# Rotation tables through one transposition in the pair of keys and values, widened by loads from DRAM, and only the rotated rows of a q result stored raw

## The chip, the cores and the metric

The kernel runs on one core of a Trainium2 chip. The metric is the device time of one execution in microseconds (us), lower is better. Before the change three executions took 894.03, 894.17 and 894.5 us; the median is 894.17.

The core has engines that run side by side, each with its own row of instructions: TensorE (PE: matrix products and transpositions), VectorE (DVE), ScalarE (ACT) and GpSimd (POOL). SyncE (SP) computes nothing here; it issues most transfers (DMAs). An engine takes its instructions strictly in order, so one that has to wait holds up all that stand behind it on the same engine.

## The reference

One block of an audio encoder over 1024 time steps and 1024 channels, all in float32. Cut to what matters:

```python
h = rmsnorm(x, norm_g[l])
proj = h @ w_in[l]                               # 1024 x 7424
q, k, v, za, u, vs, zs, gm = jnp.split(proj, IN_SPLITS, axis=-1)
q = partial_rope(q.reshape(B, S, 16, 64), pos)   # 16 heads of 64
k = partial_rope(k.reshape(B, S, 2, 64), pos)    # 2 heads
v = v.reshape(B, S, 2, 64)
a = window_sink_attention(q, k, v, att_sinks[l]) # chunks of 64, window 128
a = (a * silu(za)) @ w_att_out[l]
sgo = (chunked_spatial_gating(gelu(u), gelu(vs), ...) * silu(zs)) @ w_sg_out[l]
ga, gs = jnp.split(sigmoid(gm + b_merge[l]), 2, axis=-1)
x = rmsnorm(x + (ga * a + gs * sgo) @ w_o[l], final_g)

def partial_rope(x, pos):          # ROPE_DIM = 16: 8 angles
    ang = pos[:, None] * inv_freq[None, :]
    x1, x2, rest = x[..., :8], x[..., 8:16], x[..., 16:]
    return concatenate([x1*cos - x2*sin, x2*cos + x1*sin, rest], -1)
```

The rotation touches the first 16 of the 64 channels of a head, and uses a table of 1024 times x 8 angles of cosines and one of sines.

## The kernel before

**Pairs.** The product with `w_in` is made in pairs. A pair (`gemm_pair`) makes two blocks of 128 output channels x 1024 times with the channels on the partitions and the times along the row. It is one step of Strassen's scheme: seven products in the order b11, t1, t2, b21, t3, b22, t4, each of 12 matmuls (four slices of the sum, times three for a float32 split into a high and a low part). Keys `(n, 0..6)` name the seven weight parts of pair n. What a pair needs is made one pair ahead on the other engines: SP loads the raw weights into `wr` (`copy_to`, L212; `wr` has three buffers in rotation), DVE makes four sums of two weight blocks (tile `s`, L262 to L265: `a21+a22`, that plus `a11`, `a11+a21`, and `a12` plus the second sum), ACT rounds a part to its high half (`wh`, L176), DVE subtracts for the low half (`wl`, L177). The results of a pair are assembled from two PSUM tiles by DVE (L392, L397, L401, one for each result but the last). In the trace the product t4 writes the PSUM tile `ps_mm` that L397 has to have read.

**Stages around the change.** After the gMLP pairs comes the pair of keys and values (185.0 to 204.8 us on PE), then four pairs of q, which start on PE at 204.78 (`m=0`), 224.38 (`m=2`), 244.38 (`m=4`) and 263.42 us (`m=6`); each makes two blocks of two heads. Then come the pairs of the gate z (the first from 282.46 us), and from about 304 us the attention, step by step between the products of further pairs.

**Work beside the pairs.** `gemm_pair` calls a hook between its products. In the pair of keys and values `hook` takes steps out of the list `late`; in the q pairs `part_of_q` advances generators in `steps_of_q`: `rope_tables` in the pair `m=2`, `rotate_keys` and `rotate(0)` from `m=4`, later `first_loads` and `rotate(1)`. The order in which the instructions stand on each engine is then set by a scheduler that works on the whole program, so a changed instruction can shift others that the diff does not touch.

**The tables.** `rope_tables` loads `cos` and `sin` (times on the partitions, 16 per time step) as two DMAs into `both` (L1212), spreads the 8 angles over 8 heads by eight copies on DVE (L1218, `wide`), turns each table by four transpositions on PE (L1225, one group of four per table) and copies the PSUM tile to `tab0` and `tab1` on ACT (L1226). `tab` has 128 rows: two halves of the times, 8 heads, 8 angles.

**Results of a q pair.** `finish` stores each of the four results of a pair, 128 x 512 floats (256 KB), to `q_raw` in DRAM (`put`, L520) and the split result to `q_hl` (`split_q`, L1240 on DVE and the DMA at L1245). `rotate` later loads from `q_raw` the first 16 rows of each head (L1294), multiplies them with the tables on DVE (L1314 and after), and writes the rotated rows into `q_hl`. `rotate_keys` (L1258, L1275 to L1284) does the same for the keys out of `k_raw`, into which only the 16 rows of each of the two heads are stored (`keys_of`). The attention loads its queries from `q_hl`.

Of the kernel before, what the change touches and what calls it, by code (L numbers as in the profile page):

```python
# [24 lines left out]
F32 = mybir.dt.float32  # L25
# [5 lines left out]
P = 128  # L31
D = 1024
S = 1024
KC = D // P
HALF = 512
NT = S // P
HD = 64
# [15 lines left out]
def hybrid_tile(  # L53
# [16 lines left out]
    nc = tc.nc  # L70
# [24 lines left out]
    def xtile():  # L95
        return mtile([P, HALF], F32, "x", 5)
# [16 lines left out]
    ident = const.tile([P, P], F32, name="ident")  # L113
# [18 lines left out]
    q_raw = scratch("q_raw")  # L132
# [2 lines left out]
    k_dr = scratch("k_dr", (P, 4, S))  # L135
    v_dr = scratch("v_dr", (NT, P, 2, 3 * HD))
    s1_dr = scratch("s1_dr")
    z_dr = scratch("z_dr")
    gs_dr = scratch("gs_dr")
    ga_dr = scratch("ga_dr")  # L140
# [70 lines left out]
    def copy_to(dst, src):  # L211
        nc.sync.dma_start(dst, src)  # L212
# [11 lines left out]
    def split_next():  # L224

        if not units:
            begin_job()
        if not units:
            return
        halves, keys = units.pop(0)  # L230
        if keys[0][1] == 2:
            make_sums(term_of_x11[0] if done[0] <= 4 else None)
        hi = mtile([P, D], F32R, "wh", 3)
        lo = mtile([P, D], F32R, "wl", 3)
        if isinstance(halves, list):
            for c, half in enumerate(halves):
                split(hi[:, half_of(c)], lo[:, half_of(c)], half)
        else:
            wide = halves.shape[1]
            first = split(hi[:, 0:wide], lo[:, 0:wide], halves)  # L240
            if keys[0] == (done[0] - 1, 6) and done[0] > LAST_OF_Q + 2:
                if bounds:
                    sums_behind.append(first)
                else:
                    make_sums(first)
        of_units.append(hi_of[-1])
        for c, key in enumerate(keys):
# [106 lines left out]
    def product(acc, part, form, fresh, last=True):  # L354
        wh, wl = part
        bh, bl = form
        for k in range(4):
            ks = slice(k * P, (k + 1) * P)
            for n, (lt, rt) in enumerate(
                ((wh[:, ks], bh[:, k, :]), (wh[:, ks], bl[:, k, :]), (wl[:, ks], bh[:, k, :]))  # L360
            ):
                nc.tensor.matmul(  # L362
                    acc,
                    lt,
                    rt,
                    start=fresh and k == 0 and n == 0,
                    stop=k == 3 and n == 2,
                    skip_group_check=True,
                )

    def gemm_pair(b, finish, hook=lambda: None, second="o"):

        n = done[0]
        done[0] += 1
        acc = bank("mm")[:]
        x11, x12, x22 = xtile(), xtile(), xtile()
        product(acc, ready[n, 0], b["b11"], True)
        pace[0] = nc.scalar.copy(x11[:], acc)  # L380
        hook()
        t5 = bank("o")[:]
        product(t5, ready[n, 2], b["t1"], True)
        pace[0] = nc.scalar.mul(x22[:], t5, -1.0)
        hook()
        product(acc, ready[n, 3], b["t2"], False)
        pace[0] = nc.scalar.copy(x12[:], acc)
        split_next()
        hook()
        t2 = bank(second)[:]  # L390
        product(t2, ready[n, 1], b["b21"], True)
        term[0] = term_of_x11[0] = nc.vector.tensor_add(x11[:], x11[:], t2)  # L392
        finish(0, 0, x11, x11[:], 1.0)
        split_next()
        hook()
        product(acc, ready[n, 4], b["t3"], False)
        term[0] = nc.vector.tensor_sub(x22[:], x22[:], acc)  # L397
        finish(1, 1, x22, x22[:], 1.0)
        hook()
        product(t5, ready[n, 5], b["b22"], False)  # L400
        term[0] = nc.vector.tensor_add(x12[:], x12[:], t5)  # L401
        finish(0, 1, x12, x12[:], 1.0)
        split_next()
        hook()
        product(acc, ready[n, 6], b["t4"], False)
        finish(1, 0, xtile(), acc, -1.0)
        split_next()
        hook()
# [107 lines left out]
    def place(dst, m, half):  # L516
        return dst[m * P : (m + 1) * P, half_of(half)]

    def put(dst, m, half, src, queue=nc.sync):
        queue.dma_start(place(dst, m, half), src)  # L520
# [22 lines left out]
    pool = outer.enter_context(tc.tile_pool(name="mixing", bufs=1))  # L543
# [527 lines left out]
    late = []  # L1071
    in_twos = set()

    def hook():
        if len(late) == 1 and late[0] in in_twos:
            return
        for _ in range(2):
            if late:
                late.pop(0)()
# [57 lines left out]
    for m in range(0, KC, 2):  # L1137

        def finish(i, half, q, src, sign, m=m):
            nc.scalar.activation(q[:], src, AF.Gelu, scale=sign)  # L1140
            late.append(lambda: mix(m + i, half, q))
            in_twos.add(late[-1])
# [11 lines left out]
    pool = stage.enter_context(tc.tile_pool(name="keys", bufs=1))  # L1154
# [32 lines left out]
    def finish(i, half, q, src, sign):  # L1187
        if sign < 0:
            nc.scalar.mul(q[:], src, sign)
        (values_of if i else keys_of)(half, q)  # L1190

    gemm_pair(hb, finish, hook)
    stage.close()

# [4 lines left out]
    pool = stage.enter_context(tc.tile_pool(name="queries", bufs=1))  # L1199
    split_pool = stage.enter_context(tc.tile_pool(name="split", bufs=1))  # L1200
    SC = -(HD**-0.5)
    tables = []

    def rot_tile():
        return mtile([P, HALF], F32, "rot", 5, pool)

    both = rot_tile()[:, 0 : 2 * NT * 16].rearrange("p (f t d) -> p f t d", f=2, t=NT)

    def rope_tables():

        for f, src in enumerate((cos, sin)):
            nc.sync.dma_start(both[:, f], src)  # L1212
        yield
        for src in (both[:, 0, :, 0:8], both[:, 1, :, 8:16]):
            tab = mtile([P, HALF], F32, f"tab{len(tables)}", 1, pool)
            wide = rot_tile()
            for i in range(4):
                nc.vector.tensor_copy(  # L1218
                    wide[:, i * P : (i + 1) * P].rearrange("p (a h d) -> p a h d", a=2, h=8),
                    src[:, i : i + 5 : 4, :].unsqueeze(2).broadcast_to([P, 2, 8, 8]),  # L1220
                )
            yield
            pt = bank("tp")
            for i in range(4):
                nc.tensor.transpose(pt[:, i * P : (i + 1) * P], wide[:, i * P : (i + 1) * P], ident[:])  # L1225
            nc.scalar.copy(tab[:], pt[:])  # L1226
            tables.append(tab)
            yield

# [103 lines left out]
    for m in range(0, KC, 2):  # L1333

        def finish(i, half, q, src, sign):
            if sign < 0:
                nc.scalar.mul(q[:], src, sign)
            put(q_raw, m + i, half, q[:])
            rows = slice((m + i) * P, (m + i + 1) * P)
            split_q(q[:], [(slice(0, P), q_hl[:, rows, half_of(half)].rearrange("a p t -> p a t"))])  # L1340

        if m == 2:
            steps_of_q.append(rope_tables())
        if m == 4:
            steps_of_q.append(rotate_keys(0))
            steps_of_q.append(rotate(0, 3))
        gemm_pair(hb, finish, part_of_q)
# [62 lines left out]
    pool = stage.enter_context(tc.tile_pool(name="attention", bufs=1))  # L1410
# [234 lines left out]
    pool = stage.enter_context(tc.tile_pool(name="later", bufs=1))  # L1645
# [384 lines left out]
    for p in range(4):  # L2030
        n, t, acc, x11 = N_PAIRS + p, T_ORDER[p], accs[p], firsts[p]
# [191 lines left out]
```

## Time and profile before

The profiled execution is one execution by itself, with a time of its own.

| what | us |
|---|---|
| median of three executions | 894.17 |
| the profiled execution | 894.7 |
| its span, first to last instruction | 892.9 |
| PE busy in it | 881.7 |
| DVE busy | 684.9 |
| ACT busy | 580.1 |

The execution's time is 1.8 us longer than the span; that is what lies around the instructions. PE is busy in 99% of the span, so what other engines do appears in the time only where PE waits for it, or where PE itself has more or less to do.

A line of a timeline in the profile gives the start in us, the duration in us, engine, line of the code, operation, the tile written and the tiles read, the shapes, and a count; behind it, in brackets, the idle time of the engine ahead of it and what ended it. `DVE x L397` in a list of waits is the DVE instruction of line 397 that writes the tile `x`. SPq is SP's queue of DMA issues: its duration is that of the issue, not of the transfer.

### The profile page before, as it was taken

How to read it: one execution, taken by the hardware profiler on the slowest of the kernel's cores; microseconds unless marked ns; L12 is line 12 of the kernel's file. 1: busy time of each engine (PE TensorE's matmuls, PEld its weight loads, DVE VectorE, ACT ScalarE, POOL GpSimd, SP SyncE). 2: the span in 40 equal slices, each digit the busy share in tenths (PEclk: the TensorE clock that was granted, in tenths of full speed). 3: DMA queues.
4: the chain of work that ended last, by engine and by line, in shares of the span. 5: the costliest groups of instructions: out<-in, count | busy, mean ns of one | idle time of the engine just before them, and what ended most of it. 6: DMA issues, size and time to landing. Idle time of an engine off the chain costs nothing.

```text
span 892.9 us, 13164 instructions
## 1 busy us (share of the span) xinstructions
PE 881.7 (99%) x4117; PEld 731.4 (82%) x4117; DVE 684.9 (77%) x1362; ACT 580.1 (65%) x1189; POOL 150.9 (17%) x217
## 2 busy tenths in 40 slices
PE   8999999999999999999999999999999999999996
PEld 6888888888888888888888888888888888888885
DVE  7979966566686778888878888847796578579886
ACT  6875533334445489989989899955685385467443
POOL 3322222203030001111211011101121121110012
PEclk9999999999999999999999999999999999999999
DMA  9998888958778667888786789989899789998533
GB/s 332 211 268 222 268 206 172 176 153 265 250 252 286 214 189 189 210 185 195 179 236 210 237 225 222 250 290 383 308 289 376 276 231 258 298 307 282 179 119 118
DMA packets 131410, 212.40 MB, mean 238 GB/s; under 512 B 12778, under 2 KB 59882, under 8 KB 131340
## 3 DMA queue, kind: packets, MB, share of 16 engines
q1 hardware_dynamic: 108808, 148.62, 50.0%
q0 software_dynamic: 22384, 62.67, 31.6%
q8 instruction: 33, 0.54, 0.2%
q14 instruction: 37, 0.30, 0.1%
q10 hardware_dynamic: 148, 0.27, 0.1%
HBM read 146.37 MB, written 86.11 MB: 260 GB/s over the span
## 4 chain that ended last, share of the span: by engine, by line
PE 92%; ACT 3%; DVE 2%; issue 1%; DMA 1%; POOL 0%; SPq 0%; ACTq 0%; DVEq 0%
PE ps_mm L362 42%; PE ps_o L362 24%; PE ps_tp L362 7%; PE ps_sc L362 3%; PE ps_tp L793 2%; PE ps_o L793 2%; PE ps_mm L793 2%; PE ps_tp L1515 2%; PE ps_sc L1442 2%; PE ps_tp L1112 2%; PE ps_o L1550 1%; PE ps_sc L793 1%; ACT wh L176 1%; DVE wl L177 1%; PE ps_o L1555 1%
## 5 line engine op out<-in xcount | busy, mean ns | idle before, releaser
L176 ACT CAST wh<-s 128x1024 fp32r<-128x1024 f32 (+1 forms) x79 | 79.4, 1006 | 75.2 <-PE ps_mm L362 23.5
L177 DVE TENSOR_TENSOR wl<-wr,wh 128x512 fp32r<-128x512 f32 (+1 forms) x77 | 72.0, 937 | 58.0 <-ACT wh L176 57.9
L177 DVE TENSOR_TENSOR wl<-s,wh 128x1024 fp32r<-128x1024 f32 (+1 forms) x79 | 92.9, 1176 | 11.8 <-ACT wh L176 11.7
L176 ACT CAST wh<-wr 128x512 fp32r<-128x512 f32 (+1 forms) x77 | 63.0, 819 | 55.9 <-PE ps_mm L362 31.5
L1448 ACT COPY sl<-ps_sc 128x384 f32<-128x384 f32 (+2 forms) x128 | 51.8, 456 | 9.9 <-DVE sm L1454 9.9
L362 PE MATMUL ps_o<-T_t1h,wh 128*128 128x512 f32 x148 | 57.9, 391 | 0.0
L362 PE MATMUL ps_o<-T_t1h,wl 128*128 128x512 f32 x148 | 57.7, 390 | 0.0
L362 PE MATMUL ps_o<-T_t1l,wh 128*128 128x512 f32 x148 | 57.6, 389 | 0.0
L1470 ACT ACTIVATE pr<-pr,sm 128x192 f32<-128x192 f32 (+2 forms) x128 | 56.2, 444 | 0.1
L1454 DVE CUSTOM_DVE_ANT_0 pr<-sl,nsink_sb 128x192 f32<-128x192 f32 (+2 forms) x128 | 48.0, 399 | 9.9 <-ACT sl L1448 8.8
L362 PE MATMUL ps_mm<-T_b11h,wh 128*128 128x512 f32 x140 | 54.9, 392 | 0.0
L362 PE MATMUL ps_mm<-T_t3h,wh 128*128 128x512 f32 x140 | 54.7, 390 | 0.0
L362 PE MATMUL ps_mm<-T_b11l,wh 128*128 128x512 f32 x140 | 54.6, 390 | 0.0
L362 PE MATMUL ps_mm<-T_t2h,wh 128*128 128x512 f32 x140 | 54.6, 390 | 0.0
L362 PE MATMUL ps_mm<-T_b11h,wl 128*128 128x512 f32 x140 | 54.6, 390 | 0.0
L362 PE MATMUL ps_mm<-T_t3h,wl 128*128 128x512 f32 x140 | 54.6, 390 | 0.0
L362 PE MATMUL ps_mm<-T_t2l,wh 128*128 128x512 f32 x140 | 54.6, 390 | 0.0
L362 PE MATMUL ps_mm<-T_t3l,wh 128*128 128x512 f32 x140 | 54.5, 390 | 0.0
L362 PE MATMUL ps_mm<-T_t2h,wl 128*128 128x512 f32 x140 | 54.5, 389 | 0.0
L362 PE MATMUL ps_mm<-T_t4h,wh 128*128 128x512 f32 x136 | 53.2, 391 | 0.3 <-DVE x L397 0.3
L362 PE MATMUL ps_mm<-T_t4h,wl 128*128 128x512 f32 x136 | 53.0, 390 | 0.0
L362 PE MATMUL ps_mm<-T_t4l,wh 128*128 128x512 f32 x136 | 52.9, 389 | 0.0
(432 smaller groups left out, 2448.5 us busy)
## 6 DMA issues: line engine op xcount, KB each, us to landing
wr<-in_w_dram SPq DMA_DIRECT2D x86, 256.0 KB
sums<-in_w_dram POOLq DMA_DIRECT2D x20, 512.0 KB, 7.0
s<-sums SPq DMA_DIRECT2D x20, 512.0 KB
q_hl<-qhl SPq DMA_DIRECT2D x16, 512.0 KB
q<-q_hl SPq DMA_DIRECT2D x64, 128.0 KB
y_dr<-x POOLq DMA_DIRECT2D x28, 256.0 KB, 6.8
g<-in_w_dram POOLq DMA_DIRECT2D x12, 512.0 KB, 6.8
wr<-in_w_dram SPq DMA_DIRECT2D x11, 512.0 KB
```

The costliest lines, as they stand in the source:

```text
L176: hi_of.append(nc.scalar.copy(hi, src))
L177: lo_of.append(nc.vector.tensor_sub(lo, src, hi.bitcast(F32)))
L362: nc.tensor.matmul(acc, lt, rt, start=fresh and k == 0 and n == 0, stop=k == 3 and n == 2, skip_group_check=True,)
L793: mm = nc.tensor.matmul(acc[:], lt, rt, start=fresh and k == 0 and n == 0, stop=stops and k == 3 and n == terms[-1], skip_group_check=True,)
L1112: nc.tensor.matmul(pm[:, t * P : (t + 1) * P], xh[:, half * 4 + t, g * P : (g + 1) * P], bias[-1][1][:, g % 4, :], start=True, stop=True,)
L1442: nc.tensor.matmul(sc, q_of[:, c, i * P : (i + 1) * P], kt[:, :, lo:hi], start=True, stop=True)
L1448: copies.append(nc.scalar.copy(two, sc))
L1454: nc.vector.tensor_tensor_reduce(v, two[:, 0, :], two[:, 1, :], 1.0, nsk[:, i : i + 1], op0=ALU.add, op1=ALU.min, accum_out=nmax[:, c, i : ...
L1470: e = nc.scalar.activation(v, v, AF.Exp, bias=nmax[:, c, i : i + 1], scale=-1.0, accum_out=sums[:, c, i : i + 1])
L1515: nc.tensor.transpose(dst, pr[:, i, block * P : block * P + width], ident[:])
L1550: nc.tensor.matmul(po[:, first], va[1][:, vs], a[:, n, first], start=n == 0, stop=n == 1, skip_group_check=True)
L1555: nc.tensor.matmul(po[:, cs], vb[c][:, vs], b[c][:], start=t == 0, stop=True, skip_group_check=True)
```

## The change

Three things change.

1. The tables are turned once, in narrow form. In the pair of keys and values two DMAs load `cos` and `sin` into `both` (`load_tables`), two copies on DVE pack the 8 cosines and 8 sines of the eight time blocks into one 128 x 128 tile (`pack_tables`), one transposition on PE turns it, ACT copies the result to `turned`, and two DMAs issued by ACT write it to DRAM as `rope_dr` (2 x 8 x 1024) (`turn_tables`). These steps stand in `late`.
2. The spreading over 8 heads is done by four loads in the pair `m=2` that read the 8 rows of a half eight times (64 rows x 512 each, straight into `tab0` and `tab1`). The eight copies, the eight transpositions and the two ACT copies there are gone.
3. Of each q result only the first 16 rows of either head are stored to `q_raw`: two DMAs of 16 x 512 (32 KB) in place of one of 128 x 512.

```diff
+    rope_dr = scratch("rope_dr", (2, 8, S))
...
+    both = mtile([P, 2, NT, 16], F32, "both", 1, pool)
+    narrow, turned = (mtile([P, P], F32, tag, 1, pool) for tag in ("narrow", "turned"))
+
+    def load_tables():
+        for f, src in enumerate((cos, sin)):
+            nc.sync.dma_start(both[:, f], src)
+
+    def pack_tables():
+        for f in range(2):
+            nc.vector.tensor_copy(
+                narrow[:, 64 * f : 64 * f + 64].rearrange("p (n d) -> p n d", n=NT),
+                both[:, f, :, 8 * f : 8 * f + 8],
+            )
+
+    def turn_tables():
+        pt = bank("tp")
+        nc.tensor.transpose(pt[:, 0:P], narrow[:], ident[:])
+        nc.scalar.copy(turned[:], pt[:, 0:P])
+        for f in range(2):
+            nc.scalar.dma_start(rope_dr[f].rearrange("d (n p) -> n d p", n=NT), turned[64 * f : 64 * f + 64])
...
+    late += [load_tables, pause, pause, pause, pack_tables, pause, pause, turn_tables]
     gemm_pair(hb, finish, hook)
...
     def rope_tables():
-        for f, src in enumerate((cos, sin)):
-            nc.sync.dma_start(both[:, f], src)
-        yield
-        for src in (both[:, 0, :, 0:8], both[:, 1, :, 8:16]):
-            tab = mtile([P, HALF], F32, f"tab{len(tables)}", 1, pool)
-            wide = rot_tile()
-            for i in range(4):
-                nc.vector.tensor_copy(
-                    wide[:, i * P : (i + 1) * P].rearrange("p (a h d) -> p a h d", a=2, h=8),
-                    src[:, i : i + 5 : 4, :].unsqueeze(2).broadcast_to([P, 2, 8, 8]),
+        for f in range(2):
+            tab = mtile([P, HALF], F32, f"tab{f}", 1, pool)
+            for half in range(2):
+                nc.sync.dma_start(
+                    tab[64 * half : 64 * half + 64],
+                    rope_dr[f][:, half_of(half)].unsqueeze(0).broadcast_to([8, 8, HALF]),
                 )
-            yield
-            pt = bank("tp")
-            for i in range(4):
-                nc.tensor.transpose(pt[:, i * P : (i + 1) * P], wide[:, i * P : (i + 1) * P], ident[:])
-            nc.scalar.copy(tab[:], pt[:])
             tables.append(tab)
             yield
...
-            put(q_raw, m + i, half, q[:])
+            for g in range(2):
+                at = slice(g * HD, g * HD + 16)
+                copy_to(q_raw[(m + i) * P + g * HD : (m + i) * P + g * HD + 16, half_of(half)], q[at])
```

The scheduler's order changes with it. Line numbers after the change are higher by 1 up to the pair of keys and values and by 15 in the code of the q pairs (L262 becomes L263, L397 becomes L398, L1245 becomes L1260). Buffer numbers differ between the two orders.

The first place is PE. Before, a group of four transpositions stands between the products t2 and b21 of the pair `m=2`, and a second one between t3 and b22 (`T_t2h`, `T_b21h` and so on are the high and low parts of the activations):

```order
755 L362 MATMUL ps_mm_314_2059<-T_t2h_132_693,wh_304_2019 128x512
756 L362 MATMUL ps_mm_314_2059<-T_t2l_133_694,wh_304_2019 128x512
757 L362 MATMUL ps_mm_314_2059<-T_t2h_132_693,wl_305_2020 128x512
758 L1225 MATMUL ps_tp_323_2115<-ident_71,rot_320_2093 128x128 x4
759 L362 MATMUL ps_o_324_2121<-T_b21h_13_142,wh_300_1973 128x512
760 L362 MATMUL ps_o_324_2121<-T_b21l_14_143,wh_300_1973 128x512
```

After it, one transposition stands between b21 and t3 of the pair of keys and values, and none in the q pairs:

```order
597 L363 MATMUL ps_o_275_1782<-T_b21h_13_143,wh_250_1615 128x512
598 L363 MATMUL ps_o_275_1782<-T_b21l_14_144,wh_250_1615 128x512
599 L363 MATMUL ps_o_275_1782<-T_b21h_13_143,wl_251_1616 128x512
600 L1209 MATMUL ps_tp_279_1809<-ident_71,narrow_266_1728 128x128
601 L363 MATMUL ps_mm_268_1730<-T_t3h_139_755,wh_257_1688 128x512
602 L363 MATMUL ps_mm_268_1730<-T_t3l_140_756,wh_257_1688 128x512
```

Eight transpositions in two groups became a single one, some 150 rows earlier.

The second place is SP, from the middle of the pair `m=2` into `m=4`. Before, the raw weights of one later pair (`wr_339` and `wr_340`, four loads each) are spread between the stores of the results:

```order
75 L212 DMA wr_339_2227<-in_w_dram 128x2x128 x4
76 L1258 DMA rot_348_2257<-k_raw_90 16x1x512
77 L520 DMA q_raw_88<-x_315_2060 128x512
78 L212 DMA wr_340_2228<-in_w_dram 128x2x128 x2
79 L1245 DMA q_hl_89<-qhl_325_2136 128x2x512
80 L520 DMA q_raw_88<-x_317_2062 128x512
81 L1245 DMA q_hl_89<-qhl_330_2165 128x2x512
82 L520 DMA q_raw_88<-x_316_2061 128x512
83 L212 DMA wr_340_2228<-in_w_dram 128x2x128 x2
84 L1258 DMA rot_348_2257<-k_raw_90 16x1x512
85 L1245 DMA q_hl_89<-qhl_332_2190 128x2x512
86 L520 DMA q_raw_88<-x_335_2215 128x512
```

After it, the second raw tile (now `wr_339`) follows all stores of the pair `m=2`, the one of `qhl_335` included:

```order
72 L213 DMA wr_338_2227<-in_w_dram 128x2x128 x3
73 L213 DMA q_raw_88<-x_318_2076 16x512 x2
74 L213 DMA wr_338_2227<-in_w_dram 128x2x128
75 L1260 DMA q_hl_89<-qhl_327_2145 128x2x512
76 L213 DMA q_raw_88<-x_320_2078 16x512 x2
77 L1260 DMA q_hl_89<-qhl_330_2169 128x2x512
78 L213 DMA q_raw_88<-x_319_2077 16x512 x2
79 L1260 DMA q_hl_89<-qhl_331_2189 128x2x512
80 L213 DMA q_raw_88<-x_334_2214 16x512 x2
81 L1260 DMA q_hl_89<-qhl_335_2218 128x2x512
82 L213 DMA wr_339_2228<-in_w_dram 128x2x128 x4
```

The loads of the second tile moved from two places between the stores to one place behind them.

The third place is DVE in the pair `m=4`, which reads that tile. Before, the four sums stand ahead of the low part of `wr_311` and of the result x (L392):

```order
268 L1240 SCALAR_TENSOR_TENSOR qhl_336_2218<-x_335_2215,qhl_336_2218 128x256 x2
269 L262 TENSOR_TENSOR s_341_2237<-wr_340_2228 128x512
270 L1276 TENSOR_TENSOR rot_350_2259<-rot_348_2257,tab1_328_2145 128x512
271 L263 TENSOR_TENSOR s_341_2237<-s_341_2237,wr_339_2227 128x512
272 L1278 TENSOR_TENSOR rot_349_2258<-rot_349_2258,rot_350_2259 128x512
273 L264 TENSOR_TENSOR s_342_2238<-wr_339_2227,wr_340_2228 128x512
274 L265 TENSOR_TENSOR s_342_2238<-wr_339_2227,s_341_2237 128x512
275 L177 TENSOR_TENSOR qhl_354_2300<-rot_349_2258,qhl_354_2300 128x512
276 L177 TENSOR_TENSOR wl_353_2296<-wr_311_2048,wh_352_2295 128x512
277 L392 TENSOR_TENSOR x_344_2240<-x_344_2240,ps_o_355_2311 128x512
```

After it, two of the sums (now L263 and L265) follow that low part, and L398 (L397 before) stands eight rows behind them:

```order
267 L178 TENSOR_TENSOR wl_352_2296<-wr_314_2064,wh_351_2295 128x512
268 L263 TENSOR_TENSOR s_340_2237<-wr_339_2228 128x512
269 L265 TENSOR_TENSOR s_341_2238<-wr_338_2227,wr_339_2228 128x512
270 L393 TENSOR_TENSOR x_343_2240<-x_343_2240,ps_o_354_2311 128x512
271 L1290 TENSOR_TENSOR rot_348_2258<-rot_346_2256,tab0_321_2092 128x512
272 L178 TENSOR_TENSOR wl_357_2333<-wr_338_2227,wh_356_2332 128x1024
273 L1291 TENSOR_TENSOR rot_349_2259<-rot_347_2257,tab1_323_2109 128x512
274 L1297 TENSOR_TENSOR rot_346_2256<-rot_346_2256,tab1_323_2109 128x512
275 L1293 TENSOR_TENSOR rot_348_2258<-rot_348_2258,rot_349_2259 128x512
276 L1296 TENSOR_TENSOR rot_347_2257<-rot_347_2257,tab0_321_2092 128x512
277 L398 TENSOR_TENSOR x_345_2242<-x_345_2242,ps_mm_342_2239 128x512
```

The sums moved behind, and the other two (L264 and L266 now) come six and eight rows after the last row shown. On PE, three matmuls of the next pair's b11 also stand ahead of this pair's t4 now.

More of the change, by code (lines that the diff above doesn't have):

```diff
@@ L1190, in finish, with pause @@
         (values_of if i else keys_of)(half, q)
+    both = mtile([P, 2, NT, 16], F32, "both", 1, pool)
[15 more added lines that the diff above has]
+            nc.scalar.dma_start(rope_dr[f].rearrange("d (n p) -> n d p", n=NT), turned[64 * f : 64 * f + 64])
+    def pause():
+        pass
+    late += [load_tables, pause, pause, pause, pack_tables, pause, pause, turn_tables]
     gemm_pair(hb, finish, hook)
@@ L1205, in rot_tile @@
         return mtile([P, HALF], F32, "rot", 5, pool)
-    both = rot_tile()[:, 0 : 2 * NT * 16].rearrange("p (f t d) -> p f t d", f=2, t=NT)
     def rope_tables():
-        for f, src in enumerate((cos, sin)):
-            nc.sync.dma_start(both[:, f], src)
-        yield
-        for src in (both[:, 0, :, 0:8], both[:, 1, :, 8:16]):
-            tab = mtile([P, HALF], F32, f"tab{len(tables)}", 1, pool)
-            wide = rot_tile()
-            for i in range(4):
-                nc.vector.tensor_copy(
-                    wide[:, i * P : (i + 1) * P].rearrange("p (a h d) -> p a h d", a=2, h=8),
-                    src[:, i : i + 5 : 4, :].unsqueeze(2).broadcast_to([P, 2, 8, 8]),
-                )
-            yield
-            pt = bank("tp")
-            for i in range(4):
-                nc.tensor.transpose(pt[:, i * P : (i + 1) * P], wide[:, i * P : (i + 1) * P], ident[:])
-            nc.scalar.copy(tab[:], pt[:])
+        for f in range(2):
[4 more added lines that the diff above has]
+                    rope_dr[f][:, half_of(half)].unsqueeze(0).broadcast_to([8, 8, HALF]),
+                )
             tables.append(tab)
```

## The prediction

> **What bounds the kernel.** I read the head of the page first, then the chain that ended last, PE's list of waits, and the busy time in the pair `m=4`, 243.9 to 263.1 us (columns: PE, PEld, DVE, ACT, POOL, clock, DMA share, GB/s).
>
> ```profile
> span 892.9 us, 13164 instructions
> PE 881.7 (99%) x4117; PEld 731.4 (82%) x4117; DVE 684.9 (77%) x1362; ACT 580.1 (65%) x1189; POOL 150.9 (17%) x217
> PE 92%; ACT 3%; DVE 2%; issue 1%; DMA 1%; POOL 0%; SPq 0%; ACTq 0%; DVEq 0%
> PE ps_tp L1515 <- DVE pr L1493: 1.7, 6, 0.3
> PE ps_mm L362 <- DVE x L397: 0.3, 1, 0.3
> 243.90:263.10 19.20, 19.20 (x86) 15.90 (x85) 15.32 (x26) 8.66 (x13) 4.49 (x8) 1.00 0.77 252
> ```
>
> PE is busy 881.7 of 892.9 us and carries 92% of the chain. Its longest wait in sum outside the start is 1.7 us, far behind the stages changed here; in the pair `m=4` it is busy for all 19.20 us at full clock. So work taken off DVE, ACT or the DMA engines gives nothing here. PE work taken away counts whole, and each new wait of PE counts whole. PE's 11.2 us of idle time bound what a lighter load elsewhere could still give.
>
> **The change part by part.**
>
> *Transpositions.* I take their price from the distance of the starts of the pairs, not from their durations, because matmuls overlap. The starts, and PE around the first group:
>
> ```profile
> 224.38 0.39 PE L362 MATMUL ps_mm<-T_b11h,wh 128*128 128x512 f32 x1
> 244.38 0.39 PE L362 MATMUL ps_mm<-T_b11h,wh 128*128 128x512 f32 x1
> 263.42 0.39 PE L362 MATMUL ps_mm<-T_b11h,wh 128*128 128x512 f32 x1
> 282.46 0.39 PE L362 MATMUL ps_mm<-T_b11h,wh 128*128 128x512 f32 x1
> ...
> L1225 PE MATMUL ps_tp<-ident,rot 128*128 128x128 f32 x8 | 1.2, 272 | 0.0
> ...
> 232.54 0.60 PE L1225 MATMUL ps_tp<-ident,rot 128*128 128x128 f32 x4
> 232.90 0.48 PE L362 MATMUL ps_o<-T_b21h,wh 128*128 128x512 f32 x1
> 233.21 0.40 PE L362 MATMUL ps_o<-T_b21l,wh 128*128 128x512 f32 x1
> ...
> 332.55 0.82 PE L1515 MATMUL ps_tp<-ident,pr 128*128 128x128 f32 x6
> 333.12 0.43 PE L1442 MATMUL ps_sc<-k,q 128*128 128x384 f32 x1
> ```
>
> The pairs `m=4` and `m=6` take 263.42 - 244.38 = 19.04 and 282.46 - 263.42 = 19.04 us, which is 84 matmuls at 0.227. The pair `m=2` takes 244.38 - 224.38 = 20.00. It has the two groups and nothing else more on PE, so a group costs 0.96 / 2 = 0.48 us. The rows agree: four transpositions take 232.90 - 232.54 = 0.36, and the matmul behind them lasts 233.21 - 232.90 = 0.31 in place of 0.227, together 0.44. In the attention a group of six takes 333.12 - 332.55 = 0.57, so one more transposition costs about 0.10 us, and a single one 0.48 - 3 x 0.10 = 0.18. In all 0.18 - 0.96 = **-0.78 us**. The bounds: 7 x 0.10 = -0.7 if the start of a group cost nothing, and 7 x 0.272 = -1.90 if each gave back its own duration. I take -0.78, because it comes from starts of pairs, which are what moves the end.
>
> *Copies on DVE and ACT.* Eight copies of 1.17 us in all and two ACT copies go, two copies and one ACT copy come in the pair before. They cost and give nothing: PE waited for neither. In the pair of keys and values the transposition stands behind b21, past the middle of 19.8 us; the loads of `cos` and `sin` are issued at its start and have several us.
>
> *The tables by DRAM.* Two stores of 32 KB issued by ACT, and four loads of 128 KB by SP early in the pair `m=2`. Their user is the first product with a table on DVE, which stood at 242.46 us and now stands around 255. The lead is some 20 us, so nothing; if the path took longer than that, DVE would wait and PE behind it.
>
> *Stores to `q_raw`.* 3 MB less is written. PE does not wait for these bytes. On SP's queue 16 issues become 32 small ones:
>
> ```profile
> L520 SPq DMA_DIRECT2D q_raw<-x x16: 320/338/740, 217.5 to 285.6; - x16
> L1294 SPq DMA_DIRECT2D rot<-q_raw x8: 567/586/749, 248.0 to 295.0; - x8
> L212 SPq DMA_DIRECT2D k_raw<-x x4: 308/478/1906, 197.3 to 203.3; - x4
> SPq L212 <- DVE wl L177: 14.4, 6, 9.5
> SPq L1245 <- DVE qhl L1240: 10.0, 12, 2.2
> ```
>
> The middle one of three durations is the median in ns. The nearest row for a new store is that of `k_raw`, which is the same 16 x 512: 32 x 0.478 - 16 x 0.338 = +9.9 us of issue. The table loads have the shape of `rot<-q_raw`, 64 x 512: 4 x 0.586 = +2.3. The last two rows are SP's own longest waits from 204.8 to 301.3 us, 24.4 us in two groups alone. The additions fit into them on the whole, so 0 on the path, as long as no load that PE needs stands right behind.
>
> *The moved order.* One does. The second raw weight tile of the pair `m=6` is loaded behind the last store of the pair `m=2`; two sums on DVE read it, and L398, for which t4 of the pair `m=4` waits, stands behind them. I follow it in rows of before, shifted by -0.78:
>
> ```profile
> 226.35 0.56 SPq L212 DMA_DIRECT2D wr<-in_w_dram  x1
> 229.58 0.69 DVE L262 TENSOR_TENSOR s<-wr 128x512 f32<-128x512 f32 x1 [2.13 <-DMA wr<-in_w_dram]
> 288.43 1.91 SPq L212 DMA_DIRECT2D wr<-in_w_dram  x1
> 293.70 0.69 DVE L262 TENSOR_TENSOR s<-wr 128x512 f32<-128x512 f32 x1 [1.76 <-DMA wr<-in_w_dram]
> ...
> 233.91 2.57 SPq L212 DMA_DIRECT2D wr<-in_w_dram  x4
> 247.52 0.37 SPq L1245 DMA_DIRECT2D q_hl<-qhl  x1
> 253.16 0.69 DVE L177 TENSOR_TENSOR wl<-wr,wh 128x512 fp32r<-128x512 f32 x1 [1.50 <-ACT wh L176]
> 255.46 0.69 DVE L392 TENSOR_TENSOR x<-x,ps_o 128x512 f32<-128x512 f32 x1 [1.60 <-PE ps_o L362]
> 256.06 0.68 DVE L1281 TENSOR_TENSOR rot<-rot,tab 128x512 f32<-128x512 f32 x1
> 256.66 1.22 DVE L177 TENSOR_TENSOR wl<-wr,wh 128x1024 fp32r<-128x1024 f32 x1
> 257.80 0.75 DVE L1240 SCALAR_TENSOR_TENSOR qhl<-x,qhl 128x256 fp32r<-128x256 f32 x2
> 259.07 0.68 DVE L397 TENSOR_TENSOR x<-x,ps_mm 128x512 f32<-128x512 f32 x1
> 260.70 0.39 PE L362 MATMUL ps_mm<-T_t4h,wh 128*128 128x512 f32 x1
> 261.82 1.22 DVE L177 TENSOR_TENSOR wl<-s,wh 128x1024 fp32r<-128x1024 f32 x1
> 266.14 0.39 PE L362 MATMUL ps_o<-T_t1h,wh 128*128 128x512 f32 x1
> ```
>
> The store of `q_hl` is issued at 246.7 to 247.1; the four loads (2.57 us) end at 249.7. From the end of an issue to the sum that waited for it the first two pairs of rows give 229.58 - 226.91 = 2.67 and 293.70 - 290.34 = 3.36 us. So the weights are there at 252.4 to 253.0. On DVE the low part ahead of the sum gives way at 253.16 - 0.78 + 0.60 = 253.0. The sum is not late, but only just.
>
> From there a product or sum takes 0.60 us (256.06 to 256.66) and a wide low part 1.14 (256.66 to 257.80). The two sums end at 254.2; L393 waits for PE's product until 255.46 - 0.78 = 254.68. Behind it stand a product with a table, the low part and four more such products: L398 starts at 254.68 + 6 x 0.60 + 1.14 = 259.4 and ends at 260.1. PE would reach t4 at 260.70 - 0.78 = 259.9, and three matmuls of b11 stand ahead of it now: 260.6. The margin is 0.5 us, where before 260.70 - 259.75 = 0.95 stood. Until the low part that t1 of the pair `m=6` needs there follow, from the start of L398 at 259.4, seven products or sums of 0.60, the two late sums among them, and two low parts of q results of 0.67 (259.07 - 257.80 - 0.60): it starts at 259.4 + 4.2 + 1.3 = 264.9 and ends 1.22 later, at 266.1. Before it ended at 263.04. PE's third matmul of t1, the first that reads a low part, would run at 266.14 + 0.45 - 0.78 = 265.8, and four matmuls of b21 (0.9) stand ahead of t1 now: 266.7. The margin is 0.6, where 3.5 stood. These margins are as thin as the error of the sum. I price the waits at **+0.2 us**, between 0 and +1.0 (two thin margins missed by 0.5 each).
>
> *The sum.* The profiled execution took 894.7 us (its span and 1.8 us around it); -0.78 + 0.2 makes 894.1. The median, 894.17, is 0.5 us below that execution, so on the median the forecast is 894.17 - 0.58 = **893.6 us**, with 892.9 to 894.9 as this case's own range.
>
> **The rivals.** 0.2% of the time is 1.8 us; that is about what a measurement of this kernel can tell from no change.
>
> *Late weights (slower).* If each small store or a store of `q_hl` holds the queue longer, the weights behind them land late, both sums stand at the head of DVE and L398 with them; past 253.0 + 0.5 = 253.5 us every us is one on PE. For it speaks the third column of the row of `k_raw`, 1.906 us for the longest issue of this very size: two such in place of 0.478 are 2.9 us later on SP. The weights come at 255.3 to 255.9, and PE stalls 1.8 to 2.4 us; with the low part behind the late sums pushed as far, and its 0.5 of wait, about 2.6: 894.17 - 0.78 + 2.6 = 896.0. Against it: the median is a quarter of that, SP waits for its own producers in this stage, and bytes became fewer, with a DMA share of 0.77. It decides from a landing 3.1 us after that margin (1.8 + 0.78 = 2.6 of stall).
>
> The Trainium skill, "DMA: Bandwidth & Descriptors", section "Bandwidth", says that transfers under 64 KB are dominated by their descriptors and ought to be batched, which speaks against splitting a 256 KB store into two of 32 KB. By it the time would be this rival's; the row of `k_raw`, whose median is 0.478 us, bears it out by 0.14 us an issue only.
>
> *Dear transpositions (faster).* If each gave back its 272 ns: 894.17 - 1.90 = 892.3. The starts of pairs, 20.00 against 19.04 for eight of them, speak against it.
>
> The Trainium skill, "TensorE: Matmul & The Clock Gate", section "Part 4: PE-mode transpose", has about 275 ns for a 128 x 128 transposition inside a kernel. The row's 272 agrees as a duration; as a price by the piece it would give this rival's sum, and the distance of pairs gives less than half of it.
>
> *Relief of the transfers (faster).* With 3 MB less the waits that stand as 1.7 and 0.3 us could go: 894.17 - 0.78 - 2.0 = 891.4. The 1.7 is a wait for DVE arithmetic, so bytes do not touch it.
>
> **How the numbers follow.** The forecast's case, a small gain eaten in part by thin margins, has 0.78. Late weights have 0.14, of which 0.12 reach past 0.2%. Dear transpositions have 0.05, relief 0.03; both lie past 0.2%, the former barely, so I give faster 0.07, same 0.81, slower 0.12. The range runs from 892.3, the lower bound of the transpositions, to 895.8, inside the slower rival, where no more than 2 in 10 is left out.
>
> **What would show it.** Right: pair `m=2` lasts 19.04 us on PE, the pair of keys and values 0.18 longer than before; `m=4` starts about 243.6; no wait of PE above 0.5 us between 204 and 304; t4 of `m=4` some 16.2 us after the pair's start. Wrong: a wait of PE for L398 or for a low part in the pairs `m=4` or `m=6`, with the sum L263 ended by the transfer of `wr`; `q_raw` stores of over 1 us on SP; DVE's first product with a table waiting for its load. An attention that is 1 us longer or shorter, with the same start, would show a cause that I did not name.

## The result

Five executions of the changed kernel took 897.26 to 898.55 us, median 897.7, beside 894.17 for the kernel before (893.72 to 894.5). The ratio is 1.004 (95% interval 1.0028 to 1.0051): 3.5 us slower, where 893.6 and a range up to 895.8 stood. The profiled execution took 897.26 us.

The head of the page after, the chain that ended last, and PE's longest waits:

```profile
span 894.7 us, 13169 instructions
PE 882.4 (99%) x4110; PEld 731.0 (82%) x4110; DVE 683.6 (76%) x1356; ACT 579.1 (65%) x1188; POOL 150.8 (17%) x217
PE 91%; ACT 3%; DMA 2%; DVE 2%; issue 1%; SPq 1%; ACTq 0%; DVEq 0%
PE ps_sc L1459 <- DMA q<-q_hl: 2.6, 2, 1.5
PE ps_tp L1532 <- DVE pr L1510: 1.4, 5, 0.3
PE ps_mm L363 <- DVE x L398: 0.3, 1, 0.3
```

A new row heads PE's waits: the score products of the attention (L1459, L1442 before) wait 2.6 us for loads of queries, `q<-q_hl`. In the chain DMA has 2% in place of 1, and SP's queue 1% in place of 0.

Where the time goes shows in the starts of the pairs on PE. This table is worked out from PE's timelines: start of a product after, minus its start before, both counted from the first product of the pair of keys and values (183.94 us after, 185.03 before).

| start of (us before) | after minus before, us |
|---|---|
| `m=0` (204.78) | +0.13 |
| `m=4` (244.38) | -0.90 |
| second pair of z (301.50) | -0.80 |
| the next pair, with attention (322.81) | +0.57 |
| the one after it (347.87) | +2.89 |
| pair at 581.21 | +3.19 |
| PE's last product (885.90) | +3.24 |

The starts of `m=6` and the first z pair are left out, since there three matmuls of b11 stand ahead of the t4 of the pair before, so the start of b11 is no longer the same place. The gain of 0.90 is made, a little more than the forecast 0.78, and is kept to 301 us on the whole; 3.69 us are lost between 301 and 348. Before the pair of keys and values and behind the last product the two executions differ by another -0.7 us (-1.09 and +0.41), which makes the 2.6 between 894.7 and 897.26.

PE at the two waits, rows of its timeline after:

```profile
319.68 0.39 PE L363 MATMUL ps_mm<-T_t4h,wl 128*128 128x512 f32 x1
321.15 0.62 PE L1459 MATMUL ps_sc<-k,q 128*128 128x384 f32 x2 [1.08 <-DMA q<-q_hl]
...
332.79 0.82 PE L1532 MATMUL ps_tp<-ident,pr 128*128 128x128 f32 x6
335.09 0.59 PE L1459 MATMUL ps_sc<-k,q 128*128 128x384 f32 x2 [1.48 <-DMA q<-q_hl]
```

From the start of the row ahead to the start of the row that waits, 1.47 and 2.30 us go by where 0.23 and 0.57 would do. So the waits cost 1.24 and 1.73, together 2.97 us. The other 0.7 us of that stretch is in no row of waits. About 0.4 of it is at the group of score products at 309.77 us, which with the matmul ahead takes 0.77 where its counterpart before, at 310.20, took 0.41; and PE's order changed: of the first 14 groups of score products eight are single products between other matmuls, where before all 14 were pairs.

Before, the same two groups of score products start without a wait:

```profile
319.37 0.52 PE L1442 MATMUL ps_sc<-k,q 128*128 128x384 f32 x2
333.12 0.61 PE L1442 MATMUL ps_sc<-k,q 128*128 128x384 f32 x2
```

SP's queue tells why the queries are late. Each step of the attention needs two loads of queries; those of the third step are waited for at 321, those of the fifth at 335. First before, then after, the issues around them, from the stores of the last rotation (`q_hl<-qhl`, eight) on:

```profile
300.13 1.41 SPq L212 DMA_DIRECT2D wr<-in_w_dram  x3
303.16 5.75 SPq L1245 DMA_DIRECT2D q_hl<-qhl  x8
308.96 0.44 SPq L520 DMA_DIRECT2D z_dr<-x  x1
309.51 1.61 SPq L1389 DMA_DIRECT2D q<-q_hl  x2
...
323.00 1.25 SPq L1389 DMA_DIRECT2D q<-q_hl  x2
```

```profile
297.89 3.68 SPq L521 DMA_DIRECT2D z_dr<-x  x4
301.62 0.42 SPq L213 DMA_DIRECT2D wr<-in_w_dram  x1
306.81 5.15 SPq L1260 DMA_DIRECT2D q_hl<-qhl  x8
312.00 1.40 SPq L213 DMA_DIRECT2D wr<-in_w_dram  x3
313.45 0.43 SPq L1374 DMA_DIRECT2D k<-k_dr  x1
313.98 1.30 SPq L1406 DMA_DIRECT2D q<-q_hl  x2
...
320.24 4.56 SPq L521 DMA_DIRECT2D z_dr<-x  x3
324.85 1.87 SPq L213 DMA_DIRECT2D wr<-in_w_dram  x4
326.76 0.43 SPq L1374 DMA_DIRECT2D k<-k_dr  x1
327.32 1.24 SPq L1406 DMA_DIRECT2D q<-q_hl  x2
```

Before, the third step's loads were out by 309.51 + 1.61 = 311.12 and read at 319.37 (8.3 us later), the fifth's by 324.25 and read at 333.12 (8.9). After, they are out by 315.28 and 328.56, and PE would reach them at 319.91 and 333.36: 4.6 and 4.8 us later. The loads took up to 5.9 and 6.5 us from the end of the issue, which ends the two waits at 321.15 and 335.09. Ahead of the third step's loads now stand the rotation's stores, 3.65 us later than before because SP waits 4.7 us for their data from ACT, and three weight loads that stood ahead of those stores before. Ahead of the fifth's stand three stores of z that wait for their results, four weight loads and one of keys.

### The profile page after: what moved, and what is told of

It is laid out like the page before. It is cut to its first block, busy times and chain, and to the rows that moved or that the text cites. A ratio compares the mean times of both kernels' runs of the same rounds, so it can differ in the third digit from the quotient of the medians.

```text
span 894.7 us, 13169 instructions
## 1 busy us (share of the span) xinstructions
PE 882.4 (99%) x4110; PEld 731.0 (82%) x4110; DVE 683.6 (76%) x1356; ACT 579.1 (65%) x1188; POOL 150.8 (17%) x217
## 4 chain that ended last, share of the span: by engine, by line
PE 91%; ACT 3%; DMA 2%; DVE 2%; issue 1%; SPq 1%; ACTq 0%; DVEq 0%
PE ps_mm L363 41%; PE ps_o L363 23%; PE ps_tp L363 7%; PE ps_sc L363 3%; PE ps_o L794 3%; PE ps_mm L794 2%; PE ps_tp L794 2%; PE ps_tp L1532 2%; PE ps_sc L1459 2%; PE ps_tp L1113 2%; DMA q<-q_hl 2%; PE ps_o L1567 1%; PE ps_sc L794 1%; PE ps_sc L664 1%; DVE wl L178 1%
```

## The experiments

Three causes stood against each other: **place on SP** (two stores per result change the order of issues, and the query loads come to stand late), **small transfers** (stores of 32 KB are dear, wherever issued), and **tables by DRAM**. Each measured median below stands beside the median of the kernel before from runs on the same chip. The ratio, with its 95% interval, is taken over all executions of both and is not the quotient of the two medians. "At the end" is the last row of the table above for that kernel: its profile against before, at PE's last product. A profile is one execution, and executions of one kernel here lie up to 5.5 us apart (893.21 to 898.75 with the 80 rows below); it tells where the time goes, and the medians tell how much.

### The tables alone, and 80 rows in one store

```diff
-            for g in range(2):
-                ...                                # two stores of 16 rows
+            put(q_raw, m + i, half, q[:])          # "tables alone"
+            copy_to(q_raw[(m + i) * P : (m + i) * P + 80, half_of(half)], q[0:80])   # "80 rows"
```

> The new tables, but each q result stored whole as before (one store of 256 KB). Theory 'place on SP': with two stores per result the loads of queries for the attention come to stand behind other issues on SP, and the profile after shows PE waiting 1.24 + 1.73 us for them. Here one store per result is left, the second and third query loads of the attention are issued near 314 us as before, and only PE's 0.8 us less for transpositions is left: 893.4 (892.8 to 894.2), no wait of PE for q. Rival 'small transfers': the same, 893.4. Rival 'tables by DRAM': the new tables cost the time, 896.5 to 898.

> The new tables, and of each q result the rows 0 to 79 in one store (160 KB, the same number of issues as before, 3/8 fewer bytes). On SP the order is that of the kernel with the tables alone. Theory 'place on SP': within 0.5 us of the tables alone, near 893.4. Rival 'small transfers': the same. Rival 'bytes' (fewer bytes shift the landings, whatever the order): 1 us or more away from the tables alone, either way.

Measured: 895.71 against 894.44, ratio 1.0011 (1.0003 to 1.0020); with 80 rows 894.98, ratio 1.0011 (0.9999 to 1.0023). At the end +1.70 and +2.08. No wait for q is left in either, as the first theory says. But both times are above the expected 893.4, and the 0.8 us is not there: from -0.89 and -0.90 at `m=6` they go to +0.69 and -0.32 at the first pair of z, to +1.31 and +1.50 at the second, and rise by 0.4 and 0.6 more to the end. In `m=6` PE waits for a result once or twice (with the tables alone 0.32 us for ACT at 267.48 and 0.57 for L398 at 279.32; the rest of the 1.58 lost there is not in these rows). DVE and PE in the first pair of z, with the tables alone, then with 80 rows:

```profile
294.67 0.69 DVE L263 TENSOR_TENSOR s<-wr 128x512 f32<-128x512 f32 x1 [2.98 <-DMA wr<-in_w_dram]
298.21 0.68 DVE L398 TENSOR_TENSOR x<-x,ps_mm 128x512 f32<-128x512 f32 x1
298.95 0.50 PE L363 MATMUL ps_mm<-T_t4h,wh 128*128 128x512 f32 x1 [0.26 <-DVE x L398]
```

```profile
295.05 0.69 DVE L263 TENSOR_TENSOR s<-wr 128x512 f32<-128x512 f32 x1 [4.17 <-DMA wr<-in_w_dram]
298.59 0.68 DVE L398 TENSOR_TENSOR x<-x,ps_mm 128x512 f32<-128x512 f32 x1
299.33 0.50 PE L363 MATMUL ps_mm<-T_t4h,wh 128*128 128x512 f32 x1 [1.45 <-DVE x L398]
```

This is the mechanism of the rival "late weights", two pairs later than it was put: the sum waits for the weights at the head of DVE, L398 follows it, and PE waits for L398. It costs 0.62 and 1.82 us there. In the changed kernel it does not occur: no wait of PE stands between 200 and 321 us. The rival "tables by DRAM" had 896.5 or more; 895.71 is below that, and the loss that is there has this other cause in part.

### Two stores that carry everything

```diff
-                at = slice(g * HD, g * HD + 16)
-                copy_to(q_raw[(m + i) * P + g * HD : (m + i) * P + g * HD + 16, half_of(half)], q[at])
+                at = slice(g * HD, g * HD + HD)
+                copy_to(q_raw[(m + i) * P + g * HD : (m + i) * P + g * HD + HD, half_of(half)], q[at])
```

> The changed kernel, but the two stores of a q result carry 64 rows each (128 KB), so that all bytes of before are stored. On SP the order is that of the changed kernel. Theory 'place on SP': as slow as the changed kernel, 897 to 898.5, with PE waiting 2 us or more for q in the attention. Rival 'small transfers' (stores of 32 KB are dear): most of the loss goes, 893.5 to 895.

Measured: 898.45 against 894.44, ratio 1.0041 (1.0027 to 1.0054), +6.15 at the end; the profiled execution, 900.22, is the slowest of six. The instructions of PE, DVE, ACT and SP stand in the order of the changed kernel. In the profile PE waits 3.1 us for q in two waits. It also waits 0.51 us for L398 in `m=6`, 0.30 for a low part in the first pair of z, and 0.75 for ACT at 312.68. The loss is there without small stores: "small transfers" falls. This version is not the changed kernel with larger stores and nothing else, since its stores take SP a median of 0.596 us to issue, where the small ones take 0.419.

### The same small stores from GpSimd, and half of them

```diff
-                copy_to(q_raw[...], q[at])
+                nc.gpsimd.dma_start(q_raw[...], q[at])                          # all
+                (nc.gpsimd if g else nc.sync).dma_start(q_raw[...], q[at])      # half
```

> The changed kernel with the 32 small stores issued by GpSimd in place of SP; sizes and bytes are those of the changed kernel. On SP the order of the query loads in the attention then is that of before. Theory 'place on SP': 893.2 (892.5 to 894.2), no wait of PE for q above 0.3 us. Rival 'small transfers': 896 to 898, since the same small stores are made.

> The changed kernel, with one of the two small stores of each q result on SP and the other on GpSimd, so that SP has one store per result as before. PE's order is that of the kernel with the tables alone. Theory 'place on SP': no wait for q of 0.5 us or more; what remains is the late weight sum of the first pair of z, as with the tables alone: 895.0 (894.0 to 896.0). Rival 'small transfers': 896.5 or more.

Measured: all from GpSimd 893.7 against 894.44, ratio 0.9989 (0.9981 to 0.9998); half 894.01 against 893.94, ratio 1.0003 (0.9993 to 1.0013). At the end -0.13 and -0.33. Neither profile has a wait for q. The half keeps PE's order of the tables alone, yet it lacks that kernel's late weights: the sum in the first z pair starts at 292.80 us in place of 294.67. Its expected 895.0 was 1 us too high, at the edge of the range, because the late weights did not come.

### Only the small stores

The kernel before, with its own tables:

```diff
-            put(q_raw, m + i, half, q[:])
+            for g in range(2):
+                ...                                # two stores of 16 rows, as in the change
```

> The kernel before (tables as before, eight transpositions in the q pairs), with the two small stores of each q result on SP. On SP the second and later query loads of the attention stand behind stores of z and weight loads, as in the changed kernel. Theory 'place on SP': the waits for q are there (2.5 to 3.5 us), and the 0.8 us of the transpositions are not gained: 898.3 (897.2 to 899.3). Rival 'tables by DRAM have a part in the loss': 896.5 or less.

Measured: 898.0 against 893.94, ratio 1.0040 (1.0028 to 1.0053), +4.24 at the end. In the profile only 0.6 us of PE's waits are put down to q, where 2.5 to 3.5 were expected, and 0.4 and 0.2 to ACT; +2.09 of the loss falls between 301 and 323 us. The size of the loss is as expected, its split is not: most of it is in no row of waits, and what makes it here stays open. The new tables are not needed for the loss, so "tables by DRAM" falls: with them the profile is 0.6 to 1.0 us better.

### Queries or z results on another queue

```diff
-            nc.sync.dma_start(qt[...], rows[...])
+            nc.gpsimd.dma_start(qt[...], rows[...])      # queries from GpSimd
-            put(dst, m + i, half, q[:])
+            put(dst, m + i, half, q[:], nc.gpsimd if dst is z_dr else nc.sync)    # z from GpSimd
```

> The changed kernel, with the query loads of the attention issued by GpSimd in place of SP. Theory 'place on SP': both waits of PE for q go, the rest of the loss (score products set apart between other products, about 1 us) stays: 894.8 (893.8 to 895.8). Rival 'the data themselves are late': at least one wait of 1 us or more for q stays, 896 to 898.

> The changed kernel, with the 16 stores of the z results issued by GpSimd in place of SP; small q stores stay on SP. On SP the second query loads of the attention still stand behind the eight stores of the last rotation, the later ones no longer behind stores of z. Theory 'place on SP': the first wait of PE for q (1.2 us) stays, the second (1.7 us) goes: 896.0 (895.2 to 896.8). Rival 'the data themselves are late' (the rotated rows reach DRAM too late, whatever stands on SP): both waits stay, 897 to 898.

Measured: queries from GpSimd 894.67 against 894.2, ratio 1.0003 (0.9995 to 1.0012); z from GpSimd 893.75, ratio 0.9994 (0.9985 to 1.0002), against the same 894.2. At the end +0.23 and -0.22. The data and the small stores on SP are those of the changed kernel, and all waits for q are gone. So the rotated rows were in DRAM in time, and it was the loads that were late. GpSimd's rows with the queries on it:

```profile
305.87 1.22 POOL L1406 DMA_DIRECT2D q<-q_hl  x2 [16.96 <-PE ps_sc L1459]
312.46 1.23 POOL L1406 DMA_DIRECT2D q<-q_hl  x2 [5.38 <-PE ps_sc L1459]
321.85 1.22 POOL L1406 DMA_DIRECT2D q<-q_hl  x2 [8.16 <-PE ps_sc L1459]
328.51 1.29 POOL L1406 DMA_DIRECT2D q<-q_hl  x2 [1.80 <-PE ps_o L1567]
```

The loads of the third to fifth step go out when score products of PE have read the tile that they overwrite (the sixth's wait is put down to another product, L1567): the third's at 305.87 and the fifth's at 321.85, where SP had 313.98 and 327.32. For the z stores the expectation that the first wait stays was wrong. Without them the three weight loads moved ahead of the rotation's stores, the third step's loads went out 1.3 us earlier (2.0 us when both are counted from the pair of keys and values), and were read without a wait:

```profile
312.69 1.38 SPq L1406 DMA_DIRECT2D q<-q_hl  x2
318.53 0.59 PE L1459 MATMUL ps_sc<-k,q 128*128 128x384 f32 x2
```

Here 318.53 - 314.07 = 4.46 us from the end of the issue were enough. In the changed kernel PE came after 4.6 us and still had to wait until 5.87. So at the third step the late issue is not all: the loads were also at least 1.4 us longer under way. From the first issue to the read the DMA share was 0.99 in the changed kernel and 0.77 here. There three weight loads and one of keys go out right ahead of the queries; here the issue of these weight loads ended more than 10 us earlier. That the weight loads hold up the queries is argued, not shown: no run sets it apart from the late issue. Both come from what stands ahead in SP's queue.

Between 301 and 348 us these two still lose 0.65 and 0.5 us. Their score products are pairs again, so this is not the price of setting them apart; about 0.4 is at the same group as in the changed kernel (309.42 and 310.43 us), which with the queries on GpSimd is put down to ACT by 0.19 us. The rest stays open.

### Whole stores from GpSimd, with the old and the new tables

```diff
-            put(q_raw, m + i, half, q[:])
+            put(q_raw, m + i, half, q[:], nc.gpsimd)
```

> The kernel before, with the 16 whole stores of q results (256 KB each) issued by GpSimd in place of SP. PE's instructions stand exactly as before. Theory 'place on SP' and all others that rest on PE alone: 894.3 (893.8 to 894.9), since no wait of PE hung on these issues. Rival 'a shorter SP queue is worth something by itself': 893.3 or less, which would take away what the small stores from GpSimd gained.

> The new tables, and the 16 whole stores of q results issued by GpSimd. PE's and SP's instructions stand exactly as in the kernel with the small stores from GpSimd. Against the kernel before with its stores from GpSimd it shows the tables alone: theory -0.78 us, so 893.5 (893.0 to 894.1). Rival 'tables by DRAM': no gain, 894.3 or more. Against the small stores from GpSimd (893.7) it shows the 3 MB alone: theory 0, within 0.5 us; rival 'bytes': 1 us or more slower.

Measured: old tables 896.14 against 894.2, ratio 1.0025 (1.0016 to 1.0034); new tables 895.94, ratio 1.0019 (1.0007 to 1.0031). At the end +1.34 and +1.53. Both expectations failed. Against the small stores from GpSimd (893.7), with PE's and SP's order the same, the profiles end at -0.13 and +1.53, 1.66 us apart, and the intervals of the ratios do not overlap. The 3 MB are not the only difference, as one instruction on ACT and one on DVE also changed place. With the whole stores ACT waits for a tile that a store to `q_hl` has to free, and PE waits behind it; ACT and PE with the new tables, then ACT with the small stores:

```profile
287.32 0.66 ACT L1252 ACTIVATE qhl<-x 128x512 fp32r<-128x512 f32 x1 [3.31 <-DMA q_hl<-qhl]
287.88 0.56 ACT L381 COPY x<-ps_mm 128x512 f32<-128x512 f32 x1
288.49 0.50 PE L363 MATMUL ps_mm<-T_t2h,wh 128*128 128x512 f32 x1 [1.79 <-ACT x L381]
```

```profile
284.57 0.67 ACT L1252 ACTIVATE qhl<-x 128x512 fp32r<-128x512 f32 x1 [2.72 <-DMA q_hl<-qhl]
285.13 0.56 ACT L381 COPY x<-ps_mm 128x512 f32<-128x512 f32 x1
```

Up to `m=4` the new tables give 0.87 us here too (-0.90 against -0.03); most of what they gain is lost again to the longer wait of ACT, 1.79 in place of 1.04 us on PE. The order on ACT has a part in this. In the kernel before, the copy that PE needs stands ahead of the instruction that waits for the tile, and in the two versions here, and in that with the small stores on GpSimd, behind it. The rows before:

```profile
285.38 0.59 ACT L380 COPY x<-ps_mm 128x512 f32<-128x512 f32 x1
286.50 0.66 ACT L1237 ACTIVATE qhl<-x 128x512 fp32r<-128x512 f32 x1 [0.54 <-DMA q_hl<-qhl]
```

### Small q stores and z stores from GpSimd, and the changed kernel again

The first joins two edits shown above; the second has none.

> The changed kernel, with the small q stores and the stores of z on GpSimd. PE's and DVE's instructions stand exactly as with the small q stores alone on GpSimd, whose only loss is 0.35 us in the first pair of z and 0.4 us in the attention. Theory 'place on SP': SP is freer still, no wait for q, 893.3 (892.6 to 894.0), 0.8 us or somewhat more faster than before. Rival 'GpSimd is loaded too much': its stores come late and free their tiles late, PE waits 1 us or more for a tile of results, 894.5 or more.

> The changed kernel once more beside these: 897.7 (897.0 to 898.5), with PE waiting for q twice, 2.5 to 3.2 us in all.

Measured: both from GpSimd 893.33 against 893.94, ratio 0.9990 (0.9982 to 0.9999), -0.26 at the end; the changed kernel again 897.21, ratio 1.0041 (1.0027 to 1.0055), +3.62 at the end, with two waits of 1.6 and 1.7 us at 321.94 and 335.88. The second of these is put down to ACT L388 this time. The score products do not need that instruction: in the first profile of the changed kernel they start at 335.09, and it ends at 334.68 + 0.59 = 335.27. The order on SP is the same, and the fifth step's loads went out at 327.83. Both versions with the small stores on GpSimd are faster than before by some 0.1%, less than the 0.2% that a measurement can well tell; their intervals end just below 1.

## Why the prediction was wrong

*Transpositions: right.* -0.90 us by the starts of pairs: +0.13 in the pair of keys and values (0.18 was forecast), 242.39 - 223.35 = 19.04 us for `m=2`, as written. The dear price of 272 ns each did not come. The prediction sets 275 ns from the Trainium skill, "TensorE: Matmul & The Clock Gate", section "Part 4: PE-mode transpose", beside this row; the page gives that figure for bf16, and the tiles here are float32.

*The moved order in `m=4` and `m=6`: right.* DVE's and PE's rows after, in the order of the forecast:

```profile
251.79 0.69 DVE L263 TENSOR_TENSOR s<-wr 128x512 f32<-128x512 f32 x1
258.22 0.68 DVE L398 TENSOR_TENSOR x<-x,ps_mm 128x512 f32<-128x512 f32 x1
259.39 0.39 PE L363 MATMUL ps_mm<-T_t4h,wh 128*128 128x512 f32 x1
```

The forecast had 253.0, 259.4 and 260.6 on a shift of -0.78; this execution stands at 242.39 - 244.38 = -1.99, so 251.8, 258.2 and 259.4. The thin margin of 0.5 us held, and no wait of the price of 0.2 us came. That it held was not assured: with two stores of 128 KB and the same orders, PE waits 0.51 us for L398 and 0.30 for a low part, each one pair later than the prediction's two margins. Among the signs, "some 16.2 us" from the start of `m=4` to t4 does not fit the prediction's own sum, which gives 260.6 - 243.6 = 17.0; 259.39 - 242.39 = 17.00 was measured.

*SP's queue: the step that failed.* "The additions fit into them on the whole, so 0 on the path, as long as no load that PE needs stands right behind", and then "One does": one load was followed, the raw weights at 250 us. The query loads of the third and fifth step of the attention, 60 us later, had moved in the same queue, behind stores that wait for results and behind weight loads, and were not followed. The term put at 0 was 2.97 us of PE's time, and 0.7 more went beside it whose cause stays open. That the place on SP makes these waits is shown from both sides: with the queries on another queue (894.67) and with the z stores on another queue (893.75) they are gone. The last sign of the prediction came true, an attention that is longer from the same start by a cause not named. The issue time of the small stores does not make the loss by itself: they have a median of 0.419 us (0.478 was taken), and the same 32 on SP, with the z stores off it, give 893.75. Two of them took over 1 us (the longest 1.387), a sign of late weights in the prediction, without a stall behind them.

*Bytes: half wrong.* "PE does not wait for these bytes" holds in the profile before. Where the stores are whole and issued by GpSimd, PE waits 1.79 us behind ACT, which waits for a tile that is freed late, and the profile ends 1.66 us behind that of the small stores. How much of this is the 3 MB and how much the changed places on ACT and DVE is not shown.

*The rivals.* Late weights was a real mechanism, but at another place (the first z pair) and in other kernels (the tables alone, 80 rows). The rule of the Trainium skill, "DMA: Bandwidth & Descriptors", section "Bandwidth", that transfers under 64 KB are dominated by their descriptors, would have made the 32 KB stores the cause. The runs do not bear this out here: stores of 128 KB lose at least as much (898.45 us), and small ones from another queue nothing (893.7). Relief of the transfers did not show in the changed kernel: PE's waits of 1.7 us for DVE still stand at 1.4.

## What to carry to other kernels

Where a scheduler sets the order, splitting one transfer into two can move every later issue of that queue: compare the order of each in-order queue to the end of its reach, not only around the edit, and follow each load that the bounding engine reads. A load whose tile is free, but that stands behind stores which wait for results, is a late load; another queue for either is the cheap test. A gain on the bounding engine is real at its place and can be lost 60 us later: the starts of equal pieces of work, before against after, show where.

## What the hardware showed

A single transposition between products cost 0.13 us in the start of the next pair and two groups of four 0.96, though the rows give 272 ns for each of the eight. Loads of queries right behind three weight loads and one of keys on SP's queue held PE until 5.87 us after the end of their issue, at a DMA share of 0.99; right behind stores, at 0.77, 4.46 us were enough. With the same order on PE and SP, 3 MB less in stores went with 1.66 us less time, by a wait of ACT for a tile in the first pair of z, whose DMA share was 0.78 before: in this case the mean share did not tell when one store frees its tile.
